# A gate matvec's weights moved from the middle of a one-core kernel to its late projection units, with a transpose step reordered

## The chip, the cores and the metric

The kernel runs on one core of a Trainium2 chip. The metric is the device time of one execution in microseconds (us), lower is better. The number compared is the median of several runs.

## What is computed

One layer (DEPTH = 1) of a hybrid block over 256 latent tokens and 256 context tokens, D_MODEL 2048. The parts that matter here:

```python
shift_l, scale_l, gate_l = adaln_modulation(c, w_mod, b_mod)      # silu(c) @ w_mod + b_mod, three 2048-wide parts
h = concat([h_ctx, h_lat])                                        # modulated RMSNorm, 512 tokens
(na_q, na_k, na_v, na_gate, pool_u, pool_gate, rw_r, rw_k, rw_v, rw_gate,
 rw_lw, rw_la, merge_logits) = split(h @ w_in)                    # three mixers and the merge gates
y_na   = neighbourhood attention (16 heads of 64)                 # keys: 256 latent + 256 context
y_pool = multi-scale pooling
y_rw   = RWKV-7 scans in both directions (16 heads of 64, 64-token chunks here)
merged = sigmoid(merge_logits) parts times (branch @ w_branch), summed over three branches
out    = x_lat + gate_l * (merged @ w_out), then a final RMSNorm
```

The "gate matvec" is the last third of the first line: silu(c) times a 2048 x 2048 slice of `w_mod`, 16 MB of weights for a single output row. It is used only at the very end, in `finish`.

## The kernel before

The first stage (to about 150 us) loads x, computes shift and scale and the first seven projection tiles. Then comes the stage of the mixers (150 to about 1390 us), in which TensorE's order of work is written out by a planner; then the branch projections (`br`, to about 1526 us) and the output projection.

In the mixers' stage the bulk of the work is projection tiles. A tile is four units; a unit is one 256 KB load `raw` (line 565), a cast to `whi` on ScalarE (568), a rest `wlo` on VectorE (569), and 12 matmuls into PSUM tile `d` (738), 256 columns wide for latent tokens or 512 for all. `raw` has 7 buffers, `whi` and `wlo` 5 each. `units()` hands out units from a list `todo`, three loads ahead of the matmuls; an entry of the list is taken when its event has been reached, and entries with no event (the 48 merge tiles, and the four tiles of the gate matvec, which stand ahead of them in the list) fill whatever time is left.

Beside the units run "streams": attention for one head pair after another (`side`), and the RWKV work per head pair p (`rwkv`): `features`, `scores`, `inverse`, `merge`, `chain`, `readout`. Each stream is a generator that yields a pair (TensorE time, time until the next step is ready); `Order.run` puts up to MOST = 2.2 us of ready steps and then at least LEAST = 0.6 us of units into the order. So the constants in the yields set how much unit work stands between two dependent steps.

`scores(p, q)` (q = 0 context, 1 latent) turns v into `pv` (230), copies it to `SV` by four ScalarE copies (235), then makes the score products `pb` and `pk` from `BK` and `EO` (248, 250), masks them on VectorE (253 to 268), and last transposes `BK` for both heads, eight transposes of head 0 into one PSUM tile `pt`, then eight of head 1 into another (276), with a ScalarE copy after each (277). All of these PSUM tiles share two buffers (tag "f"). `BK` itself is finished by `features` on VectorE (210) and ScalarE (211).

A tile of the gate matvec (`gate_tile`, 952 to 980) is 16 loads `wg` of 256 KB (957) into the `raw` buffers, [128, 512] with 2 KB rows. After each four loads follow four matmuls of 512 columns (967), one in each group of 32 columns of the array; after 16 the copy `gs` (972), the sum over the four groups `pg` (946), an add into `gb` (947) and a store to `gd` (948).

After the mixers, `bload` brings the three branches back: one buffer `bf` of 1 MB is loaded (1039), cast to `bh` on ScalarE (1042), and its rest `bl` made on VectorE (1043), three times in a row. The first matmuls of `br` need `bh0` and `bl0`, the next ones `bh1`, `bl1`, then `bh2`, `bl2`.

Of the kernel before, what the change touches and what calls it, by code (L numbers as in the profile page):

```python
# [9 lines left out]
F32 = mybir.dt.float32  # L10
# [9 lines left out]
class Rwkv:  # L20
# [90 lines left out]
    def features(s, p, q, zk, zv, T, psp, ptag, gates):  # L111


        nc, fp = s.nc, s.fp
        nm = f"{p}_{q}"
# [10 lines left out]
        k = s.mix(zk, 0, p, "k" + nm)  # L126
# [21 lines left out]
        h = 0.5 * C  # L148
# [63 lines left out]
        s.BK, s.v = BK, v  # L212
        yield 0.0, 2.6

# [6 lines left out]
    def scores(s, p, q, psp, ptag):  # L221
# [9 lines left out]
        for par in range(2):  # L231
            h = hv[1 - par]
            for d in range(2):
                o = SV[h, par, ::-1, d] if d else SV[h, par, :, d]
                nc.scalar.copy(o, pv[h])
        yield 0.6, 1.6
        v4 = lambda a: a.rearrange("p (e c) t -> p e c t", e=2)
        for g in range(1 + q):
# [25 lines left out]
            else:  # L264
                m = (s.mb, s.mk1)[g]
                for par in range(2):
                    r = hv[1 - par]
                    nc.vector.tensor_tensor(v4(EO[r, par, g]), v4(pk[r]), m[r].unsqueeze(2).to_broadcast([64, 2, 4, 64]), ALU.mult)
            yield 1.7, (2.5 if g == q else 2.2)
        s.blocks_out(p, q)  # L270

        for par in range(2):
            pt = psp.tile([128, 8, 64], F32, tag=ptag, name=f"pt{nm}_{par}")
            for c in range(8):
                src = BK[hv[par], c, par:par + 2, :].rearrange("p a t -> p (a t)")
                nc.tensor.transpose(pt[:, c], src, s.ident[hv[par], hv[par]])
            nc.scalar.copy(s.BKT[p, q][:, par], pt.rearrange("p (d c) t -> p d c t", d=2))
        yield 1.3, 0.0

# [73 lines left out]
    def chain(s, p, psp, ptag, psy, ytag, y, mark):  # L353
# [6 lines left out]
        for i in range(8):  # L360
# [16 lines left out]
            if q:  # L377
                py = psy.tile([128, 2, 64], F32, tag=ytag, name=f"py{p}_{i}")
                for d in range(2):
                    for par in range(2):  # L380
                        nc.tensor.matmul(py[hv[par], d], SV[:, par, w, d], EO[:, par, d, 4 + cs[d], :], start=(d == 0), stop=False,
                                         tile_position=(0, 64 * par), skip_group_check=True)
            yield (0.9 if q else 0.45), (0.6 if q else 1.0)
            pu = psp.tile([128, 2, 64], F32, tag=ptag, name=f"pu{p}_{i}")
# [3 lines left out]
            for par in range(2):  # L388
                (nc.scalar.copy if par else nc.vector.tensor_copy)(SV[hv[par], par, w], pu[hv[par]])
            yield 0.4, 1.3  # L390
            if i < 7:
# [139 lines left out]
def hybrid_block(ctx, tc, x, cx, w_ms, w_st, w_in, w_mg, w_br, w_out, pool_w, icnt, wa, bias, rows, params, out, dbg=None):  # L531
    nc = tc.nc
    mark = (dbg or {}).get("mark", lambda *_: None)
    P = 128
# [212 lines left out]
    with ExitStack() as mx:  # L747
# [121 lines left out]
        def attention(p):  # L869
# [10 lines left out]
            for qt in range(2):  # L880
# [35 lines left out]
                nc.vector.scalar_tensor_tensor(g[:, c], po, 0.5, g[:, c], ALU.mult, ALU.mult)  # L916
                yield 1.1, 0.3
            keep(0, p, g)
# [23 lines left out]
        def gate_out(cc, gs, gb):  # L942
            yield 0.0, 1.2
            c = slice(512 * cc, 512 * cc + 512)
            pg = psd.tile([P, 512], F32, tag="d", name=f"pg{cc}")
            nc.tensor.matmul(pg, selg, gs, start=True, stop=True)
            nc.vector.tensor_tensor(gb, pg, gb, ALU.add)
            nc.sync.dma_start(gd[:, c], gb)
            yield 1.1, 0.0

        def gate_tile(cc):

            wgs, box = {}, []

            def unit_(u):
                wg = wgs[u] = wp.tile([P, 512], F32, tag="raw", bufs=NRAW, name=f"wg{cc}_{u}")
                nc.sync.dma_start(wg, w_mg[cc, u // 2, :, u % 2])
                if u % 4 < 3:
                    return []

                def mult():
                    if not box:
                        box.append(psd.tile([P, 512], F32, tag="d", name=f"mg{cc}"))
                    a = box[0]
                    for kt in range(u - 3, u + 1):
                        g = kt % 4
                        nc.tensor.matmul(a[32 * g:32 * g + 32], cs[:, kt], wgs[kt], start=(kt < 4), stop=(kt >= 12),
                                         tile_position=(0, 32 * g))
                    if u == 15:
                        gs = wp.tile([P, 512], F32, tag="raw", bufs=NRAW, name=f"gs{cc}")  # L970
                        gb = wp.tile([P, 512], F32, tag="raw", bufs=NRAW, name=f"gb{cc}")
                        nc.scalar.copy(gs, a)
                        nc.sync.dma_start(gb, rows[0:1, 512 * cc:512 * cc + 512].to_broadcast([P, 512]))
                        O.add(gate_out(cc, gs, gb), 1)
                    return 1.4
                return [mult]
            return [lambda u=u: unit_(u) for u in range(16)]

# [4 lines left out]
        for p in range(8):  # L983
# [12 lines left out]
            if p % 2:  # L996
                for e in range(2):
                    todo.append((f"at{p}", tile_(PL_U + p - 1 + e, True, pool_u, p // 2, e)))
                for e in range(2):
                    todo.append((f"at{p}", gate_(PL_G + p - 1 + e, f"plg{p - 1 + e}", "g2p", 2)))  # L1000
            if p >= 4:
                todo.append((None, lambda cc=p - 4: gate_tile(cc)))
        for i in range(48):
            todo.append((None, tile_(MERGE + i, True, merge_out, i)))

        def units():

            ready, cur = [], []
            while True:
                while len(ready) < AHEAD:  # L1010
                    if not cur:
                        i = next((i for i, (ev, _) in enumerate(todo) if ev is None or O.has(ev)), None)
                        if i is None:
                            break
                        cur = todo.pop(i)[1]()
                    ready.append(cur.pop(0)())
                if not ready:
                    if not todo:
                        return
                    yield None  # L1020
                    continue
                for m in ready.pop(0):
                    yield m()
# [161 lines left out]
```

## Time and profile before

| | us |
|---|---|
| median of 3 runs (lowest to highest) | 1617.97 (1617.08 to 1625.06) |
| profiled execution, its own time | 1624.09 |
| its span, first to last instruction | 1622.2 |
| TensorE (PE) busy | 1544.7 |
| VectorE (DVE) busy | 1140.2 |
| ScalarE (ACT) busy | 813.6 |
| granted TensorE clock, mean | 0.990 |

PE is TensorE's matmuls, PEld its weight loads, SP the engine that issues the DMAs. A profile row gives the start or the busy time first, then the engine, the line of the kernel, the operation and its tiles. A busy PE need not be at its peak: ends of matmuls are modelled, and a group of matmuls in which one waits for a load still counts as busy in part. A wait is put down to the event that came last.

### The profile page before, as it was taken

What the parts mean: (1) busy time and instruction counts of PE and PEld (TensorE: products, weight loads), DVE (VectorE), ACT (ScalarE), POOL (GpSimd) and SP (SyncE); (2) the same over time, 40 slices, a digit from 0 to 9 for tenths busy, and PEclk for the clock granted to TensorE, in tenths of its full rate; (3) what the DMA queues carried; (4) which work ended last, traced back from release to release, by engine and by line L of the source; (5) the groups of instructions that cost most, each with busy time, mean ns of one, the idle gap of its engine ahead of it and who ended that gap; (6) DMA issues with size and microseconds to landing.
All of it is one profiled execution on the core that took longest, in us unless ns stands there. A gap on an engine that the chain in (4) does not pass through costs nothing.

```text
span 1622.2 us, 36488 instructions
## 1 busy us (share of the span) xinstructions
PE 1544.7 (95%) x13848; PEld 1314.9 (81%) x13848; DVE 1140.2 (70%) x2585; ACT 813.6 (50%) x1604; POOL 248.5 (15%) x441
## 2 busy tenths in 40 slices
PE   6999989899999998998999999999899999999998
PEld 4667747388887887877888897787799999999987
DVE  4334875588688788778768878968886554677774
ACT  5224732455364466446446546536644554444553
POOL 2222200140031023023014214003312100000000
PEclk9999999999999999999999999999999999999999
DMA  9997376754433433442442452342366486677892
GB/s 380 331 337 237 111 224 201 231 166 156 144 99 104 146 111 107 134 125 73 137 125 85 153 173 86 105 147 83 106 184 191 163 259 231 221 231 233 271 310 74
DMA packets 201617, 283.26 MB, mean 175 GB/s; under 512 B 67809, under 2 KB 97633, under 8 KB 196833
## 3 DMA queue, kind: packets, MB, share of 16 engines
q1 hardware_dynamic: 201440, 280.93, 53.7%
q8 instruction: 109, 1.79, 0.4%
q14 instruction: 68, 0.55, 0.1%
HBM read 262.24 MB, written 18.35 MB: 173 GB/s over the span
## 4 chain that ended last, share of the span: by engine, by line
PE 78%; DVE 8%; DMA 5%; ACT 4%; issue 3%; SPq 1%; POOL 0%; ACTq 0%; DVEq 0%
PE d L738 43%; PE br L574 3%; PE br L575 3%; PE br L576 3%; PE acc L662 2%; PE psm L614 2%; PE o L574 2%; PE o L575 2%; PE o L576 2%; DMA wg<-in_w_mg 2%; PE acc L665 2%; PE acc L668 2%; DVE wlo L569 2%; DMA bf<-bs 1%; PE pu L387 1%
## 5 line engine op out<-in xcount | busy, mean ns | idle before, releaser
L738 PE MATMUL d<-hh,whi 128*128 128x256 f32 (+1 forms) x1952 | 573.7, 318 | 2.4 <-ACT whi L568 2.2
L568 ACT CAST whi<-raw 128x512 fp32r<-128x512 f32 x584 | 358.5, 620 | 421.8 <-PE d L738 287.5
L738 PE MATMUL d<-hl,whi 128*128 128x256 f32 (+1 forms) x1952 | 553.1, 307 | 0.0
L569 DVE TENSOR_TENSOR wlo<-raw,whi 128x512 fp32r<-128x512 f32 x584 | 404.0, 700 | 175.2 <-ACT whi L568 125.9
L738 PEld LDWEIGHTS d<-hh,whi 128*128 128x128 f32 x1952 | 369.8, 189 | 35.6 <-issue 5.6
L738 PEld LDWEIGHTS d<-hl,whi 128*128 128x128 f32 x1952 | 370.5, 190 | 17.6 <-issue 0.2
L738 PE MATMUL d<-hh,wlo 128*128 128x256 f32 (+1 forms) x1952 | 365.5, 308 | 2.9 <-DVE wlo L569 2.8
L738 PEld LDWEIGHTS d<-hh,wlo 128*128 128x128 f32 x1952 | 287.1, 190 | 22.3 <-DVE wlo L569 3.9
L369 POOL TENSOR_SCALAR sg<-SV,G 64x64 f32<-64x64 f32 x192 | 107.3, 564 | 275.2 <-DVE SV L404 139.5
L574 PE MATMUL br<-bh,whi 128*128 128x256 f32 x384 | 107.9, 281 | 0.0
L575 PE MATMUL br<-bl,whi 128*128 128x256 f32 x384 | 107.9, 281 | 0.0
L576 PE MATMUL br<-bh,wlo 128*128 128x256 f32 x384 | 107.9, 281 | 0.0
L308 DVE TENSOR_TENSOR iM<-iA,iT 128x126 f32<-128x126 f32 (+22 forms) x248 | 65.2, 263 | 12.1 <-DMA iA<-dA 5.6
L576 PEld LDWEIGHTS br<-bh,wlo 128*128 128x128 f32 x384 | 72.4, 188 | 0.0
L574 PEld LDWEIGHTS br<-bh,whi 128*128 128x128 f32 x384 | 72.4, 188 | 0.0
L575 PEld LDWEIGHTS br<-bl,whi 128*128 128x128 f32 x384 | 72.4, 188 | 0.0
L310 DVE TENSOR_TENSOR iT<-iT,iM 128x126 f32<-128x126 f32 (+22 forms) x248 | 64.2, 259 | 6.4
L675 ACT ACTIVATE hh<-xT,md 128x256 fp32r<-128x256 f32 x32 | 17.5, 594 | 88.9 <-DVE md L634 88.9
L1113 DVE TENSOR_TENSOR hl<-rawo,hh 128x512 fp32r<-128x512 f32 x64 | 42.6, 689 | 21.8 <-ACT hh L1112 21.5
L1112 ACT CAST hh<-rawo 128x512 fp32r<-128x512 f32 x64 | 39.3, 621 | 33.2 <-DMA rawo<-in_w_out 15.9
L575 PE MATMUL o<-hl,mh 128*128 128x512 f32 (+1 forms) x144 | 52.6, 366 | 0.0
L574 PE MATMUL o<-hh,mh 128*128 128x512 f32 (+1 forms) x144 | 52.6, 365 | 0.0
(283 smaller groups left out, 2286.6 us busy)
## 6 DMA issues: line engine op xcount, KB each, us to landing
raw<-in_w_in SPq DMA_DIRECT2D x488, 256.0 KB, 3.3
wm<-in_w_ms SPq DMA_DIRECT2D x32, 1024.0 KB, 6.8
raw<-in_w_br SPq DMA_DIRECT2D x96, 256.0 KB, 3.2
wg<-in_w_mg SPq DMA_DIRECT2D x64, 256.0 KB, 4.6
rawo<-in_w_out SPq DMA_DIRECT2D x64, 256.0 KB, 4.3
wst<-in_w_st SPq DMA_DIRECT2D x16, 448.0 KB, 7.5
md__79<-mth SPq DMA_DIRECT2D x48, 128.0 KB, 2.7
mth<-md__79 SPq DMA_DIRECT2D x48, 128.0 KB, 3.1
```

Source lines behind the costliest of these rows:

```text
L308: nc.vector.tensor_tensor(m, A[:, st:st + 1, st + 1:32].to_broadcast([128, ni, nt]), T[:, 0:ni, st:st + 1].to_broadcast([128, ni, nt]), AL ...
L310: nc.vector.tensor_tensor(T[:, 0:ni, st + 1:32], T[:, 0:ni, st + 1:32], m, ALU.add)
L369: nc.gpsimd.tensor_scalar(sg[hv[par], d], SV[hv[par], par, w, d], G[hv[par], gs[d][0], d:d + 1], None, ALU.mult)
L568: nc.scalar.copy(h, raw)
L569: nc.vector.tensor_tensor(l, raw, h.bitcast(F32), ALU.subtract)
L574: nc.tensor.matmul(acc, a[0], b[0], start=start, stop=False)
L575: nc.tensor.matmul(acc, a[0], b[1], start=False, stop=False)
L576: nc.tensor.matmul(acc, a[1], b[0], start=False, stop=stop)
L614: mm = nc.tensor.matmul(psm[j][32 * g:32 * g + 32, 0:256], cs[:, kt], wm[:, k], start=(kt < 4), stop=(kt >= 12), tile_position=(0, 32 * g))
L738: nc.tensor.matmul(box[0], w[m >= 8][:, 128 * i:128 * i + 128], x, start=(u == 0 and m == 0), stop=(u == 3 and m == 11))
L1112: nc.scalar.copy(hh[kt], raw)
L1113: nc.vector.tensor_tensor(hl[kt], raw, hh[kt].bitcast(F32), ALU.subtract)
```

## The change

Three things. (1) The gate matvec no longer has tiles of its own in `todo`. Its weights come in 64 pieces [128, 2, 256] of 256 KB (rows of 1 KB), into four buffers that attention used (`kt`, `PT`), one piece with each projection unit that is handed out after attention and pooling of the last pair are over (event `side7`). After each second piece follow four matmuls of 256 columns. `gs` and `gb` move into attention's `sl` buffers, and the PSUM tiles into attention's. (2) In `scores` the transposes stand ahead of the score products, and the two heads alternate. (3) Constants in yields are changed.

```diff
 features:
-        yield 0.0, 2.6
+        yield 0.0, (3.6 if q == 0 else 4.8)
 scores:
                 nc.scalar.copy(o, pv[h])
-        yield 0.6, 1.6
+        yield 0.6, 1.2
+
+        pt = [psp.tile([128, 8, 64], F32, tag=ptag, name=f"pt{nm}_{par}") for par in range(2)]
+        for c in range(8):
+            for par in range(2):
+                src = BK[hv[par], c, par:par + 2, :].rearrange("p a t -> p (a t)")
+                nc.tensor.transpose(pt[par][:, c], src, s.ident[hv[par], hv[par]])
+        for par in range(2):
+            nc.scalar.copy(s.BKT[p, q][:, par], pt[par].rearrange("p (d c) t -> p d c t", d=2))
+        yield 0.9, 1.6
...
-            yield 1.7, (2.5 if g == q else 2.2)
+            yield 1.3, 2.6
         s.blocks_out(p, q)
-
-        for par in range(2):
-            pt = psp.tile([128, 8, 64], F32, tag=ptag, name=f"pt{nm}_{par}")
-            for c in range(8):
-                src = BK[hv[par], c, par:par + 2, :].rearrange("p a t -> p (a t)")
-                nc.tensor.transpose(pt[:, c], src, s.ident[hv[par], hv[par]])
-            nc.scalar.copy(s.BKT[p, q][:, par], pt.rearrange("p (d c) t -> p d c t", d=2))
-        yield 1.3, 0.0
 chain:
-            yield (0.9 if q else 0.45), (0.6 if q else 1.0)
+            yield (0.9 if q else 0.45), (0.7 if q else 1.2)
...
-            yield 0.4, 1.3
+            yield 0.4, 1.6
 attention:
-                yield 1.1, 0.3
+                yield 1.1, 1.0
 gate_out:
-            pg = psd.tile([P, 512], F32, tag="d", name=f"pg{cc}")
+            pg = psn.tile([P, 512], F32, tag="o", name=f"pg{cc}")
-        def gate_tile(cc):
...
-                wg = wgs[u] = wp.tile([P, 512], F32, tag="raw", bufs=NRAW, name=f"wg{cc}_{u}")
-                nc.sync.dma_start(wg, w_mg[cc, u // 2, :, u % 2])
-                if u % 4 < 3:
+        def gate_units():
...
+            def load(cc, h, k):
+                wg = np_.tile([P, 2, 256], F32, tag=("kt", "PT")[k // 2 % 2], bufs=2, name=f"wg{cc}_{h}_{k}")
+                nc.sync.dma_start(wg, w_mg[cc, k, :, :, 256 * h:256 * h + 256])
+                held.append(wg)
+                if k % 2 == 0:
                     return []
...
+                    for i in range(4):
+                        kt = 2 * k - 2 + i
                         g = kt % 4
-                        nc.tensor.matmul(a[32 * g:32 * g + 32], cs[:, kt], wgs[kt], start=(kt < 4), stop=(kt >= 12),
-                                         tile_position=(0, 32 * g))
+                        nc.tensor.matmul(a[32 * g:32 * g + 32], cs[:, kt], held[i // 2][:, i % 2], start=(kt < 4), stop=(kt >= 12),
+                                         tile_position=(0, 32 * g), skip_group_check=True)
...
-                    return 1.4
+                    return 0.75
 todo:
-            if p >= 4:
-                todo.append((None, lambda cc=p - 4: gate_tile(cc)))
 units:
                         cur = todo.pop(i)[1]()
+                        if O.has("side7") and gates:
+                            cur = [lambda u=u, g=gates.pop(0): u() + g() for u in cur]
```

How the order of instructions moves, at three places.

TensorE, gate matvec. Before, the matmuls `mg` of a gate tile stand among the attention and RWKV steps of pairs 0 and 1 (`po`, `pg`, `S`), with no unit between (here the last gate tile):

```order
L946 MATMUL pg2_3150<-gs2_3136,selg_128 128x512
L967 MATMUL mg3_3162<-wg3_0_3128,cs_74 32x512
L967 MATMUL mg3_3162<-wg3_1_3130,cs_74 32x512
L967 MATMUL mg3_3162<-wg3_2_3154,cs_74 32x512
L967 MATMUL mg3_3162<-wg3_3_3156,cs_74 32x512
L887 MATMUL S1_0_1_3169<-kh1_2707,qh1_2602 128x512
```

Now they stand between the units of the last 20 projection tiles, a pair of pieces after every second unit (`d109` is a merge tile, `whi410` belongs to unit 410 of 488):

```order
L739 MATMUL d109_15987<-hh6_87,wlo410_15954 128x256
L739 MATMUL d109_15987<-hh7_88,wlo410_15954 128x256
L970 MATMUL mg0_16024<-wg0_0_0_15933,cs_74 32x256 x2
L970 MATMUL mg0_16024<-wg0_0_1_15957,cs_74 32x256 x2
L739 MATMUL d109_15987<-hh8_89,whi411_15981 128x256
L739 MATMUL d109_15987<-hl8_105,whi411_15981 128x256
```

The first pair follows unit 410, the last one unit 472; 16 units are left after it, and then `br` begins.

TensorE, the transposes of `scores` for pair 7, q = 1. Before, they come after `pb` and `pk`, head after head:

```order
L738 MATMUL d39_15061<-hh2_83,whi353_14973 128x256
L738 MATMUL d39_15061<-hl2_99,whi353_14973 128x256
L276 MATMUL pt7_1_0_15072<-ident_63,BK7_1_14610 128x64 x8
L276 MATMUL pt7_1_1_15082<-ident_63,BK7_1_14610 128x64 x8
L738 MATMUL d39_15061<-hh3_84,whi353_14973 128x256
```

Now they come between `pv` and `pb`, one of head 0 and one of head 1 in turn, sixteen rows of which these are the first:

```order
L739 MATMUL d39_15533<-hh2_83,wlo393_15427 128x256
L739 MATMUL d39_15533<-hh3_84,wlo393_15427 128x256
L242 MATMUL pt7_1_0_15556<-ident_63,BK7_1_15208 128x64
L242 MATMUL pt7_1_1_15557<-ident_63,BK7_1_15208 128x64
L242 MATMUL pt7_1_0_15556<-ident_63,BK7_1_15208 128x64
L242 MATMUL pt7_1_1_15557<-ident_63,BK7_1_15208 128x64
```

Between `pv` and the first transpose of head 1 stand 12 to 20 unit matmuls in most of the 16 cases, and between the last transpose and `pb` about as many.

SP, the first load of `bload`. Before, `bf0` is issued soon after the last RWKV result `grwg7` is stored, with 52 units still to load:

```order
L764 DMA bs_80<-grwg7_15261 128x256 [waits DMAHW1_49,DVE_49]
L565 DMA raw433_17030<-in_w_in 128x512 [waits DMAHW2_49,DVE_49]
L565 DMA raw434_17048<-in_w_in 128x512 [waits DMAHW3_49,DVE_49]
L565 DMA raw435_17069<-in_w_in 128x512 [waits DMAHW4_49,DVE_49]
L829 DMA md__79<-mth31_16914 128x256 [waits DMAHW5_49,Activation_49]
L565 DMA raw436_17088<-in_w_in 128x512 [waits DMAHW6_49,DVE_49]
L1039 DMA bf0_18137<-bs_80 128x8x256 [waits DMAHW7_49,PE_49,Pool_49]
```

Now it stands behind the store of the last gate part (`gd` from `gb3`) and waits for that queue slot (DMAHW3), with one unit left to load:

```order
L977 DMA gb3_17886<-in_rows 128x512 [waits DMAHW0_49]
L566 DMA raw484_18064<-in_w_in 128x512 [waits DMAHW1_49,DVE_49]
L566 DMA raw485_18082<-in_w_in 128x512 [waits DMAHW2_49,DVE_49]
L949 DMA gd_78<-gb3_17886 128x512 [waits DMAHW3_49,DVE_49]
L566 DMA raw486_18100<-in_w_in 128x512 [waits DMAHW4_49,DVE_49]
L566 DMA raw487_18121<-in_w_in 128x512 [waits DMAHW5_49,DVE_49]
L1044 DMA bf0_18201<-bs_80 128x8x256 [waits DMAHW6_49,DMAHW3_49,PE_49]
```

## Rows read from the trace of the kernel before

**Rows 1.** The page: busy time, share of the span and instructions of each engine; then the chain of work that ended last, shares of the span by engine.
```profile
PE 1544.7 (95%) x13848; PEld 1314.9 (81%) x13848; DVE 1140.2 (70%) x2585; ACT 813.6 (50%) x1604; POOL 248.5 (15%) x441
...
PE 78%; DVE 8%; DMA 5%; ACT 4%; issue 3%; SPq 1%; POOL 0%; ACTq 0%; DVEq 0%
```

**Rows 2.** Busy time by stretch: from:to, its length, then busy us (instructions) of each engine, granted clock in the stretch, mean busy share of the 16 DMA engines, GB/s.
```profile
200.00:325.00 125.00, 110.90 (x832) 67.68 (x831) 76.10 (x189) 46.00 (x97) 5.38 (x18) 0.97 0.69 215
...
900.00:1050.00 150.00, 147.20 (x1408) 123.38 (x1407) 123.20 (x302) 84.88 (x172) 33.06 (x53) 1.00 0.42 127
...
1296.00:1332.00 36.00, 33.91 (x278) 32.92 (x277) 18.45 (x23) 19.39 (x31) 0.00 (x0) 1.00 0.83 271
```

**Rows 3.** Waits of TensorE's matmuls from 150 to 1390 us: who waited for whom, us in total, times, longest.
```profile
PE pb L250 <- DVE BK L210: 8.9, 5, 2.4
PE mg L967 <- DMA wg<-in_w_mg: 6.7, 8, 1.4
PE S L887 <- DVE gnag L916: 4.6, 4, 1.8
PE pS L397 <- ACT SV L389: 4.4, 7, 1.6
PE pu L387 <- DVE xs L376: 4.1, 7, 1.2
PE pg L946 <- ACT gs L972: 3.6, 3, 1.5
...
PE pb L250 <- ACT BK L211: 3.2, 5, 0.8
...
PE pk L248 <- ACT SV L235: 0.8, 1, 0.8
...
PE pk L250 <- ACT SV L235: 0.3, 1, 0.3
```

**Rows 4.** The gate matvec's matmuls (line 967) alone: the last line of the busy time by stretch from 200 to 325 us (sum over the stretches); then, from the view of tile `wg`, the time from issue to landing of its loads.
```profile
sum 125.00, PE 37.41 PEld 6.13; mean PE 6.23 PEld 1.02
...
DMA to landing us min/median/max: 2.5/4.6/6.6
```

**Rows 5.** Timeline of TensorE at the gate matvec: start, length, instruction, count, and the idle time ahead of it with its releaser.
```profile
207.75 1.06 PE L967 MATMUL mg<-wg,cs 128*32 128x512 f32 x8
208.74 0.66 PE L905 MATMUL pt<-ident,sl 128*128 128x128 f32 x4
...
305.34 1.05 PE L967 MATMUL mg<-wg,cs 128*32 128x512 f32 x4
307.71 1.72 PE L967 MATMUL mg<-wg,cs 128*32 128x512 f32 x4 [1.32 <-DMA wg<-in_w_mg]
309.36 0.50 PE L887 MATMUL S<-kh,qh 64*128 64x512 f32 x2
```

**Rows 6.** Timeline of TensorE in the first stage, where the shift and scale matvec (`psm`) has the shape that the gate matvec will have.
```profile
23.31 1.93 PE L614 MATMUL psm<-wm,cs 128*32 128x256 f32 x32
...
30.75 0.40 PE L662 MATMUL acc<-hh,shi 128*128 128x512 f32 x1
30.99 0.40 PE L665 MATMUL acc<-hh,slo 128*128 128x512 f32 x1
31.22 0.63 PE L668 MATMUL acc<-hl,shi 128*128 128x512 f32 x2
31.78 1.07 PE L614 MATMUL psm<-wm,cs 128*32 128x256 f32 x16
32.78 0.50 PE L662 MATMUL acc<-hh,shi 128*128 128x512 f32 x1
33.12 0.40 PE L665 MATMUL acc<-hh,slo 128*128 128x512 f32 x1
```

**Rows 7.** Timeline of TensorE: attention scores, whose two heads alternate, and behind them one set of 16 transposes of line 276.
```profile
218.04 0.39 PE L887 MATMUL S<-kl,qh 64*128 64x512 f32 x2
218.27 0.40 PE L887 MATMUL S<-kh,ql 64*128 64x512 f32 x2
218.51 0.95 PE L276 MATMUL pt<-ident,BK 64*128 64x64 f32 x16
219.40 1.93 PE L967 MATMUL mg<-wg,cs 128*32 128x512 f32 x8
```

**Rows 8.** The view of line 235 (copies of `pv` to `SV`): duration in ns, min/median/max.
```profile
L235 ACT COPY SV<-pv x64: 348/367/370, 178.4 to 1156.4; 64x256 f32<-64x256 f32 x64
```

**Rows 9.** Timelines: the end of the last gate tile (ScalarE, TensorE, VectorE, SP); then `bload` from the issue of `bf0` to the last `bl`. Last, the DMA view's line of the stores to `gd`: count, KB each, median us to landing.
```profile
321.71 0.58 ACT L972 COPY gs<-mg 128x512 f32<-128x512 f32 x1
...
325.41 0.33 SPq L948 DMA_DIRECT2D gd<-gb  x1
...
1296.72 0.38 SPq L1039 DMA_DIRECT2D bf<-bs  x1
...
1329.64 2.29 DVE L1043 TENSOR_TENSOR bl<-bf,bh 128x2048 fp32r<-128x2048 f32 x1 [5.57 <-ACT bh L1042]
...
gd<-gb SPq DMA_DIRECT2D x4, 256.0 KB, 3.0
```

**Rows 10.** Busy time by stretch, columns as in rows 2: merge units alone; `bload` beside units (two stretches); the gate matvec's loads; the stores of the inverse and the loads of its result; then, from the DMA view, the line of the x loads (count, KB each, median us to landing).
```profile
1340.00:1385.00 45.00, 45.00 (x383) 45.00 (x382) 21.78 (x33) 22.39 (x41) 0.00 (x0) 1.00 0.67 221
...
1296.70:1305.50 8.80, 8.80 (x76) 8.80 (x76) 3.46 (x5) 2.94 (x7) 0.00 (x0) 1.00 0.96 311
...
1321.00:1327.00 6.00, 6.00 (x53) 6.00 (x52) 3.07 (x6) 1.08 (x2) 0.00 (x0) 1.00 0.96 276
...
290.00:300.00 10.00, 7.42 (x45) 2.47 (x41) 2.44 (x8) 1.46 (x3) 1.74 (x4) 1.00 0.84 237
...
1209.60:1212.40 2.80, 2.80 (x26) 2.80 (x25) 2.67 (x5) 1.48 (x3) 0.00 (x0) 1.00 0.94 213
1212.50:1216.40 3.90, 3.90 (x36) 3.90 (x35) 0.23 (x1) 1.57 (x4) 0.00 (x0) 1.00 0.70 170
...
xt<-in_x SPq DMA_DIRECT2D x2, 1024.0 KB, 10.1
```

More of the change, by code (lines that the diff above doesn't have):

```diff
@@ L949, in gate_out @@
             yield 1.1, 0.0
-        def gate_tile(cc):
-            wgs, box = {}, []
-            def unit_(u):
-                wg = wgs[u] = wp.tile([P, 512], F32, tag="raw", bufs=NRAW, name=f"wg{cc}_{u}")
-                nc.sync.dma_start(wg, w_mg[cc, u // 2, :, u % 2])
-                if u % 4 < 3:
+        def gate_units():
+            held = []
+            def load(cc, h, k):
[3 more added lines that the diff above has]
+                if k % 2 == 0:
@@ L959, in unit_ @@
                     return []
                 def mult():
[L962 to L965, printed above, removed]
-                        g = kt % 4
-                        nc.tensor.matmul(a[32 * g:32 * g + 32], cs[:, kt], wgs[kt], start=(kt < 4), stop=(kt >= 12),
-                                         tile_position=(0, 32 * g))
[L969 to L972, printed above, removed]
+                    if h == 0 and k == 1:
+                        T["mg"] = psn.tile([P, 512], F32, tag="s", name=f"mg{cc}")
@@ new lines, in mult @@
+                    a = T["mg"][:, 256 * h:256 * h + 256]
+                    for i in range(4):
+                        kt = 2 * k - 2 + i
+                        g = kt % 4
+                        nc.tensor.matmul(a[32 * g:32 * g + 32], cs[:, kt], held[i // 2][:, i % 2], start=(kt < 4), stop=(kt >= 12),
+                                         tile_position=(0, 32 * g), skip_group_check=True)
+                    del held[0:2]
+                    if h == 1 and k == 7:
+                        gs = np_.tile([P, 512], F32, tag="sl", bufs=2, name=f"gs{cc}")
+                        gb = np_.tile([P, 512], F32, tag="sl", bufs=2, name=f"gb{cc}")
+                        nc.scalar.copy(gs, T["mg"])
@@ L973, in mult @@
                         nc.sync.dma_start(gb, rows[0:1, 512 * cc:512 * cc + 512].to_broadcast([P, 512]))
                         O.add(gate_out(cc, gs, gb), 1)
-                    return 1.4
+                    return 0.75
                 return [mult]
-            return [lambda u=u: unit_(u) for u in range(16)]
+            return [lambda cc=cc, h=h, k=k: load(cc, h, k) for cc in range(4) for h in range(2) for k in range(8)]
         todo = []
@@ L1006, in units @@
         def units():
-            ready, cur = [], []
+            ready, cur, gates = [], [], gate_units()
             while True:
@@ L1018, in units @@
                     if not todo:
+                        assert not gates
                         return
```

## The prediction

> **What bounds the kernel now.** I read the page first, then the busy time by stretch, the waits of TensorE, and the timelines at the places that the change touches. TensorE is busy for 1544.7 of 1622.2 us and makes 78% of the chain that ended last [rows 1]. So a change gains what it takes from TensorE's own time or from the holes in it. Unit work without an event is always at hand to fill holes, but only where the written order puts it. The stretch from 200 to 325 us is the weakest of the mixers' stage: 110.90 busy of 125, against 147.20 of 150 from 900 to 1050 [rows 2]. In it lies the whole gate matvec.
>
> The sum is made against the profiled execution, 1624.09 us. The median of the runs shown is 6.1 us (0.4%) lower, and I carry the difference over. A measurement of this kernel can tell about 0.5% (8 us) from no change.
>
> **Gate matvec, taken out of 200 to 325 us.** Its matmuls fill 37.4 us [rows 4]; TensorE is idle for 6.7 us more until a `wg` load lands and 3.6 us until `gs` is copied [rows 3]. Together 47.7 us. Much of the 37.4 is waiting too: with its data there a group of four matmuls takes 1.0 us (207.75 to 208.74), while another takes 4.0 (305.34 to 309.36) [rows 5], so 16 groups need only some 16 us. Removed: 47.7.
>
> **Gate matvec, put back between late units.** 32 pairs of pieces, each four matmuls of 256 columns. The trace before has this shape only in `psm`. There eight matmuls (16 records) start 0.09 us late (31.78, where 31.22 + 0.24 + 0.23 was due), take 1.00 us, and the next interval is 0.34 instead of 0.23: 1.20 us per visit. Another group with 32 records takes 1.93 instead of 1.07, so eight records fewer save 0.43 [rows 6]. A pair then costs 0.77 us and 32 of them 24.5. The ends: 0.43 without any cost at the edges (14 us) and 1.0, the group of 512 columns (32 us). I take the `psm` row, which is the same shape. The Trainium skill (TensorEngine Tiling (Array Packing), Key Properties) says that changing the tiling mode drains TensorE, which speaks against cutting the matvec into twice as many visits; the late start and the long interval in `psm` agree with it. Without that rule, by the body of the group alone, the sum would gain about 6 us more. To the 24.5 I add 2 us for the four `pg`, each of which waits about half a us for its `gs` (0.58 us [rows 9]) half a unit behind the last pair. Net of the two parts: 47.7 - 24.5 - 2 = **21.2 saved**.
>
> **Transposes.** A set of 16 takes 0.89 us (218.51 to 219.40), one after another. Attention's scores have the same split of the rows into two halves and alternate heads: there a pair of 512-column matmuls takes 0.23 us (218.04 to 218.27) [rows 7], as much as a single one of that width in rows 6 (30.75 to 30.99). If the two halves overlap as they do there, each of the 16 sets loses half: 16 x 0.445 = **7.1 saved**. The ends are 0 and 7.1; I take the upper one because the row is the same tile shape.
>
> **More units ahead of the waits.** Behind `BK` the first step that needs it stood 2.6 + 0.6 + 1.6 = 4.8 us later by the planner's count; for q = 1 it is now 4.8 + 0.6 + 1.2 = 6.6. The waits on `BK` are 8.9 and 3.2 us, five each, longest 2.4 [rows 3]; 1.8 us more ahead of them removes about **9** (0 to 12). The waits for `gnag`, `SV` and `xs` are 4.6, 4.4 and 4.1 us [rows 3]; their yields grow by 0.7, 0.3 and 0.1 to 0.2 us, and I count **4** (0 to 13).
>
> **A new wait.** The second PSUM buffer for the transposes is that of `pv`, and comes free after four copies of 0.37 us, 1.5 us in all [rows 8], plus whatever ScalarE has ahead of them (a cast of 0.62). Before, `pk` met the same wait, for only 0.8 and 0.3 us [rows 3], with more units ahead. Now 12 unit matmuls of 0.1175 us (45 us / 383 [rows 10]), 1.4 us, often stand there. Behind the waiting transpose stands all of TensorE. 16 times 0.4 is **6 lost** (0 to 13).
>
> **The late units and their loads.** From unit 409 to 472 TensorE has 64 units of 12 x 0.1175 = 1.41 us (90 us), the 24.5, and some 19 us of `pg`, the last pair's chain, merge and readout (an estimate of mine, by their groups' counts): 134 us, or 4.2 per pair of units. The DMAs have 128 loads of 256 KB, 16 stores of 128 KB and six transfers for `gb` and `gd`: 37.2 MB, and the inverse of pair 7, whose last two steps fill all engines for 2.6 and 2.7 us (0.94 x 2.8, 0.70 x 3.9 [rows 10]); with its first steps about 8, an estimate. The pieces have rows of 1 KB, as `bf` has. Beside `bf` the DMAs moved 311 GB/s at a share of 0.96 and 276 at 0.96, beside units alone 221 at 0.67 [rows 10], that is 324, 288 and 330 at full share. So the loads need 115 to 129 us plus 8, 123 to 137, against TensorE's 134. They are about level, so the loads no longer hide in all stretches: **6 lost** (0 to 31, the upper end in a rival below). The Trainium skill (DMA: Bandwidth & Descriptors, Specifications) puts the smallest transfer for line rate at 512 B, so by it 1 KB rows cost nothing, and at 330 GB/s this term would be 0; the row with 276 GB/s at 0.96 says otherwise, and I go by the rows.
>
> **What is late next: `bload`.** Before, `bf0` was issued at 1296.72 with over 50 units left, and the last `bl` was done 35.2 us later (1329.64 + 2.29) [rows 9] with only 2.1 us of idle TensorE (36 - 33.91 [rows 2]). Now `bf0` waits for the store of the last gate part. That store was issued at 325.41, 3.7 us after `gs` began at 321.71, and takes 3.0 to land [rows 9]: with the drain before `gs`, `bf0` starts 7.1 us after the last pair, and `bl2` is done at 7.1 + 35.2 = 42.3. TensorE has left 16 units (22.6), `pg` (0.6), and the first two branches' 48 matmuls (5.7), 28.9 us. It misses 13.4; less the 2.1 lost before: **11.2 lost** (5 to 17). Nothing can fill this, since all units are used up.
>
> **Sum.** Saved 21.2 + 7.1 + 9 + 4 = 41.3, lost 6 + 6 + 11.2 = 23.2: 18.1 us. 1624.09 becomes 1606.0, and on the runs' level 1617.97 - 18.1 = **1600 us**.
>
> **Rivals.**
> - *The tail costs nothing.* Loads stay ahead and units still cover `bload`. For: TensorE and DMAs are level in the middle estimate, and raw loads run some ten units ahead. Against: `bf0` really stands behind `gd` in SP's order. Then 17.2 us more are saved: 1583.
> - *The loads set the pace of the tail.* The old gate loads, issued in a row, moved only 237 GB/s from 290 to 300 us [rows 10]. At that rate 37.2 MB take 157 us, with the inverse 165, 31 more than TensorE's 134 in place of 6: the sum becomes +6.9, or 1625, no change that can be told. The moved weights would give back what the middle gained.
> - *Slower: the loop of four buffers.* A pair of pieces can be loaded only when the pair before the last has been multiplied, so two pairs pass per landing plus 0.77. At the landing times of before (median 4.6, longest 6.6 [rows 4]) that is under 4.2 us per pair and costs nothing. Two loads of raw and two of `wg` now share the queue, though, and 1 MB x loads in the busy first stage took 10.1 us to land [rows 10]. At 10.1 a pair takes 5.44, 1.25 more than 4.19: 40 us instead of 6, so the sum is 15.8 slower, 1634. It decides from a landing of 9.1 us on, where the other terms' 24.1 us are used up (24.1 / 32 = 0.75 per pair). Against it: the DMAs catch up while TensorE waits.
> - *The change doesn't do what it says* in one part: the two halves' transposes don't overlap. Then 7 less, 1607; this stays inside the forecast's own range.
>
> **How the numbers follow.** The forecast with its bounds (1588 to 1611): 0.47, nearly all of it faster by over 0.5% (below 1609.9). The free tail: 0.17, faster. The loads' pace: 0.20, within 0.5%. The slower loop: 0.13, and 0.03 for something else on that side, half of it within. So faster 0.63, same 0.23, slower 0.14. The range runs from 1581, just below the free tail, to 1625, the loads' pace; beyond it lie the slower loop and a few hundredths of a better outcome.
>
> **What would show it.** Right: from 200 to 325 us TensorE is over 97% busy and no row of `wg` is left there; pairs of `mg` take about 0.8 us; sets of transposes take 0.45; waits on `BK` fall below 4 us; the idle time ahead of `br` lies with `bf`, `bh` or `bl` and is 9 to 15 us; `wg` lands in 4 to 7 us. Wrong: over 20 us of TensorE's idle time put down to `wg`, a landing over 9 us, or a transposes' wait of more than 0.8 us each on `SV`. If `br` begins without a wait, the term for `bload` was wrong.

## The result and the profile after

The changed kernel takes 1595.37 us (median of 4 runs, 1594.43 to 1598.03) beside 1618.68 for the kernel before (4 runs): a ratio of 0.9851, 95% interval 0.9822 to 0.9881. That is 23.3 us faster by the medians. The profiled execution of it takes 1594.74 us, that of before 1624.09, so the two traces differ by 29.4 us; 5.4 of these are the profiled execution of before being above its median.

The page of the changed kernel, busy time and then the chain that ended last:

```profile
PE 1520.5 (95%) x13976; PEld 1309.4 (82%) x13976; DVE 1132.3 (71%) x2585; ACT 815.9 (51%) x1606; POOL 242.3 (15%) x441
...
PE 78%; DVE 9%; DMA 5%; ACT 4%; issue 2%; POOL 1%; SPq 1%; ACTq 0%; DVEq 0%; POOLq 0%
```

Beside [rows 1] the bound is the same: TensorE is busy for 24.2 us less in a span 29.2 us shorter. Busy time by stretch, columns as in [rows 2]:

```profile
200.00:325.00 125.00, 122.15 (x1282) 109.96 (x1281) 104.95 (x253) 70.18 (x149) 16.34 (x36) 1.00 0.49 149
...
1332.00:1480.00 148.00, 139.19 (x1152) 138.26 (x1152) 102.60 (x180) 70.28 (x116) 0.00 (x0) 0.98 0.75 236
```

The weak stretch has become full (110.90 before), with 450 more instructions of TensorE in the same 125 us. A new hole of 8.8 us has opened behind 1332. Waits of TensorE's matmuls from 150 to 1400 us, columns as in [rows 3]:

```profile
PE br L575 <- ACT bh L1047: 5.6, 1, 5.6
PE mg L970 <- DMA wg<-in_w_mg: 5.2, 5, 2.1
PE pt L242 <- DVE BK L210: 4.8, 2, 3.5
PE pk L259 <- DVE EO L277: 3.6, 4, 1.4
PE pS L398 <- ACT SV L390: 3.5, 3, 1.5
PE pu L388 <- DVE xs L377: 3.1, 6, 0.7
...
PE pt L242 <- ACT SV L235: 2.8, 4, 1.4
...
PE pt L242 <- ACT BK L211: 1.7, 3, 0.7
PE br L576 <- DVE bl L1048: 1.5, 1, 1.5
...
PE S L888 <- DVE gnag L917: 0.3, 1, 0.3
```

The waits on `BK` stand with the transposes now and fell from 12.1 to 6.5; `gnag` fell from 4.6 to 0.3. The two at `br` (7.1) are new; with 1.7 us just ahead of it (`whi` and `wlo` late at 1344 and 1346 us) they are the 8.8. All waits from 150 to 1400 us sum to 53.4 us before and 48.0 after. So most of the difference between the traces is TensorE's own time: its busy time on the gate's products fell from 37.4 to 25.5 us and on the transposes from 18.8 to 14.4, and the clock, below, cost 6.6 us less.

One visit to a pair of gate pieces in TensorE's timeline:

```profile
1320.61 0.39 PE L739 MATMUL d<-hh,wlo 128*128 128x256 f32 x2
1320.93 0.64 PE L970 MATMUL mg<-wg,cs 128*32 128x256 f32 x8
1321.50 0.39 PE L739 MATMUL d<-hh,whi 128*128 128x256 f32 x1
1321.72 0.28 PE L739 MATMUL d<-hl,whi 128*128 128x256 f32 x1
```

Two unit matmuls from 1320.61 would have let the pair start at about 1320.84; it starts 0.09 late, takes 0.57, and the next interval is 0.22 instead of 0.12. That makes 0.76 us, as `psm` in [rows 6] let expect (0.77). The Trainium skill (TensorEngine Tiling (Array Packing), Key Properties) has TensorE drain at a change of the tiling mode; the two longer intervals agree with it.

The end of the gate matvec, SP's timeline of the changed kernel, and then VectorE's one row there that waits:

```profile
1325.48 1.00 SPq L977 DMA_DIRECT2D gb<-in_rows  x1
1326.58 2.40 SPq L566 DMA_DIRECT2D raw<-in_w_in  x2
1330.76 0.33 SPq L949 DMA_DIRECT2D gd<-gb  x1
1331.36 0.93 SPq L566 DMA_DIRECT2D raw<-in_w_in  x2
1333.44 0.38 SPq L1044 DMA_DIRECT2D bf<-bs  x1
```

```profile
1330.04 0.69 DVE L948 TENSOR_TENSOR gb<-pg,gb 128x512 f32<-128x512 f32 x1 [1.42 <-DMA gb<-in_rows]
```

The last pair begins at 1324.54, and `bf0` is issued 8.9 us behind that. Some of it is `gb` itself: its load is issued only behind the last pair and lands 4.6 us later.

What the prediction has no term for is TensorE's clock. Busy time of TensorE by stretch (then granted clock, DMA share, GB/s), first in the kernel before, then in the changed one:

```profile
230.00:232.00 2.00, 1.20 (x8) 0.92 0.95 342
232.00:234.00 2.00, 1.49 (x7) 0.50 0.93 329
234.00:236.00 2.00, 2.00 (x11) 0.50 0.35 122
236.00:238.00 2.00, 2.00 (x10) 0.50 0.21 68
```

```profile
1360.00:1362.00 2.00, 0.00 (x0) 0.92 1.08 370
1362.00:1364.00 2.00, 0.00 (x0) 0.50 1.04 377
1364.00:1366.00 2.00, 1.72 (x8) 0.50 0.84 310
1366.00:1368.00 2.00, 2.00 (x11) 0.50 0.06 23
1368.00:1370.00 2.00, 2.00 (x17) 0.87 0.19 67
```

Both fall to the lower level (0.50, which is 1.2 of 2.4 GHz) behind a wait: at 230 TensorE had stood for 1.82 us, at 1362 it stands in the 5.6 us for `bh`. Work goes on at half speed for some us after the wait has ended. I took such stretches one us at a time from 150 to 1500 us and summed busy time times (1 - granted clock): 12.8 us in the kernel before, 6.2 in the changed one. The Trainium skill (TensorE: Matmul & The Clock Gate, Part 1) lets half or all of the clock through by how busy the array has lately been; these rows agree.

The 6.6 us between them are a matter of these two executions, though, and not of the two kernels. Every execution's mean granted clock is on record: 0.991 to 0.993 in the four of the changed kernel, and a median of 0.992 (0.985 to 0.995) in the 43 of the kernel before that the runs below were timed against. The profiled one of before has 0.990.

### The profile page after: what moved, and what is told of

Same layout as the page of the kernel before. It is cut to its first block, busy times and chain, and to the rows that moved or that the text cites. A ratio compares the mean times of both kernels' runs of the same rounds, so it can differ in the third digit from the quotient of the medians.

```text
span 1593.0 us, 36719 instructions
## 1 busy us (share of the span) xinstructions
PE 1520.5 (95%) x13976; PEld 1309.4 (82%) x13976; DVE 1132.3 (71%) x2585; ACT 815.9 (51%) x1606; POOL 242.3 (15%) x441
## 4 chain that ended last, share of the span: by engine, by line
PE 78%; DVE 9%; DMA 5%; ACT 4%; issue 2%; POOL 1%; SPq 1%; ACTq 0%; DVEq 0%; POOLq 0%
PE d L739 43%; PE br L575 3%; PE br L577 3%; PE br L576 3%; PE acc L663 2%; PE psm L615 2%; PE o L577 2%; PE o L575 2%; PE o L576 2%; DMA wg<-in_w_mg 2%; PE acc L669 2%; PE acc L666 2%; DVE wlo L570 1%; PE pu L388 1%; DMA bf<-bs 1%
## 5 line engine op out<-in xcount | busy, mean ns | idle before, releaser
L1117 ACT CAST hh<-rawo 128x512 fp32r<-128x512 f32 x64 | 39.5, 621 | 33.0 <-PE o L577 23.3
L624 DVE COPY ms<-psm 128x256 f32<-128x256 f32 x16 | 6.8, 425 | 65.1 <-PE psm L615 65.1
```

Source lines behind the costliest of these rows:

```text
L1117: nc.scalar.copy(hh[kt], raw)
```

## Experiments

Each was timed beside the kernel before on its chip (1620.1 to 1621.7 us there); ratios are to it.

**The parts, one at a time.** Four runs: the gate's edits alone, the rest of the change alone, the new order of the scores alone, the other pauses alone. Their edits, hunks of the change on top of the kernel before (`e2` on the change, with the gate's undone):

```
e1 (the reverse of this, on the change, is e2)
-            if p >= 4:
-                todo.append((None, lambda cc=p - 4: gate_tile(cc)))
+            ready, cur, gates = [], [], gate_units()
...
+                        if O.has("side7") and gates:
+                            cur = [lambda u=u, g=gates.pop(0): u() + g() for u in cur]
e3
-        yield 0.6, 1.6
+        yield 0.6, 1.2
+        pt = [psp.tile([128, 8, 64], F32, tag=ptag, name=f"pt{nm}_{par}") for par in range(2)]
...
-            yield 1.7, (2.5 if g == q else 2.2)
+            yield 1.3, 2.6
e4
-        yield 0.0, 2.6
+        yield 0.0, (3.6 if q == 0 else 4.8)
-            yield (0.9 if q else 0.45), (0.6 if q else 1.0)
+            yield (0.9 if q else 0.45), (0.7 if q else 1.2)
-            yield 0.4, 1.3
+            yield 0.4, 1.6
-                yield 1.1, 0.3
+                yield 1.1, 1.0
```

> The kernel before with the gate matvec's weights moved to the late units and nothing else (scores and yields as before). My theory, with the terms as the changed kernel's profile shows them: 47.7 us of gate work and waits leave the middle, 24.5 + 2 come back late, about 5 us of waits on wg and 7 us of bload are lost, so 9 to 13 us faster than before. Rival A (the late loads eat the whole gain, and the gain of the change comes from the reordered scores and the yields): within 4 us of before. Rival B (the gate move is the whole gain): 20 to 25 us faster.

> The changed kernel with the gate matvec back in the middle as four tiles of its own; transposes of scores and all yields stay changed. My theory: 10 to 15 us faster than before (fewer waits on BK, gnag, SV, xs). Rival A: 20 to 25 us faster, all of the gain. Rival B: within 4 us of before.

> The kernel before with scores as in the change (transposes of both heads in turn, ahead of the score products, with the yields inside scores), all other yields and the gate as before. If alternating heads overlapped, 16 sets would lose half of 0.89 us and it would be 5 to 7 us faster. The changed kernel's profile shows a set at 0.94 us still, so my theory now is no gain from the overlap, and waits on BK that move from pb to pt: within 3 us of before.

> The kernel before with only the yields of features, chain and attention changed; scores and gate as before. My theory: the waits on BK (12 us), gnag, SV and xs (13 us) shrink, 8 to 14 us faster. Rival: these waits are replaced by others of the same length, within 3 us of before.

Gate alone: 0.9916 (0.9888 to 0.9944), 13.6 us faster. The rest: 0.9908 (0.9891 to 0.9924), 14.9. Order: 0.9952 (0.9936 to 0.9969), 7.8; this I had expected to be nothing, from a set of 0.94 us that in fact holds a wait for `SV` behind its first transpose (at 1148.7 us in the changed kernel; most sets without a wait take 0.59 to 0.73). Pauses: 1.0001 (0.9987 to 1.0015), nothing, where I had expected 8 to 14. So gate and rest both count, and add up within the noise (28.5 beside 24.2 for the change by its ratio).

Why the pauses alone take nothing off can be read from the waits of `e4`:

```profile
PE mg L967 <- DMA wg<-in_w_mg: 9.9, 10, 2.0
...
PE pb L250 <- ACT BK L211: 2.5, 5, 0.7
...
PE pb L250 <- DVE BK L210: 2.2, 2, 1.5
```

The waits that the pauses were meant for did fall: on `BK` from 12.1 to 4.7 us, on `gnag`, `SV` and `xs` together from 13.1 to 5.3. But others grew, on `wg` from 6.7 to 9.9, and all of them from 150 to 1400 us sum to 53.2 beside 53.4. The rival held. And the granted clock is lower, 0.987 to 0.990 (median 0.989) in all 11 executions of `e4`; the trace has 16.2 us lost to it, 12.8 before. With the order, the pauses came out 7 ahead of the order alone (`e2` beside `e3`); the runs below return to that.

**The gate's price in both kernels.** The matvec left out of the changed kernel (`e6`) and of the kernel before (`e7`); the gate row then holds its bias alone.

```
-            ready, cur, gates = [], [], gate_units()
+            ready, cur, gates = [], [], []
...
+            nc.sync.dma_start(gb, rows[0:1, 512 * cc:512 * cc + 512].to_broadcast([P, 512]))
+            nc.sync.dma_start(gd[:, 512 * cc:512 * cc + 512], gb)
```

> The changed kernel without the gate matvec: the gate row holds its bias alone and is written at the start, so 256 products, their 64 loads and the row's sums are left out. My theory (the gate costs its own 32 pair visits of 0.76 us, 24.3 us, five waits of 5.2 us on pieces and about 6 us of the wait for the bias row at the end): 33 to 38 us faster than the changed kernel, 1557 to 1562 us beside 1595. Rival (the gate's products stand in gaps that TensorE would spend waiting for other engines): under 25 us. Other rival (its 16.8 MB also delay the projection's loads): over 42 us.

> The kernel before without the gate matvec, left out in the same way. My theory (there the gate costs its four groups at 11.9 us each, 47.7 us, and 2.1 us at the end): 46 to 51 us faster than the kernel before, about 1570 us. Then the gate's price has fallen by 13 us from the kernel before to the changed one, as the gate alone moved did in its own run. Rival (the groups partly fill waits of attention): under 38 us, and then the gain of moving the gate comes from elsewhere.

`e7`: 0.9714 (0.9690 to 0.9737), so the gate costs 46.4 us in the kernel before (47.2 by the medians, 1574.49 beside 1621.73). `e6`: 0.9612 (0.9593 to 0.9630), 1558.94; against the change's 0.9851 that is 38.8 us, some 6 either way by the intervals, a little over the 33 to 38 expected and far from the 25 of the first rival.

The parts can be found in the traces. The 32 visits make 24.3 and the sums over bands 4.4 busy. Late pieces cost about twice the 5.2 us that the matmuls' waits show, since the modelled ends of the matmuls cover the rest: the weight loads ahead of them (PEld) waited for 10.1 us (the changed kernel's view of tile `wg`), and the visits that met a late piece were longer by about that much.

```profile
  PEld mg L970: 10.1, 12
```

Of the 8.8 us at the end 4.9 go, since without a gate TensorE still waits at `br` for 3.9. But `e6` has 4.8 us in two casts where the mixers' stage begins, behind its early loads of the gate's rows (last row; the change has none there). `e7` has such a wait too.

```profile
PE br L575 <- ACT bh L1052: 2.5, 1, 2.5
...
PE br L576 <- DVE bl L1053: 1.4, 1, 1.4
...
PE d L739 <- ACT whi L569: 4.8, 2, 3.7
```

Together 24.3 + 4.4 + 10.1 + 4.9 - 4.8 = 38.9. The price fell by 7.6 us, beside 9 from `e2` to the change: the visits save some 23 us, and the late pieces and the end take most of that back. The gate alone gained more (13.6); with the old pauses, 480 unit matmuls stand behind the last pair, and `br` begins without a wait for `bh` or `bl`.

**The pauses.** The changed kernel with the old pause behind the features (`e13`), and with all four pauses of the list of `e4` at their old values (`e14`).

```
e13
-        yield 0.0, (3.6 if q == 0 else 4.8)
+        yield 0.0, 2.6
e14, the same line and the other three pairs of e4 reversed
-            yield 0.4, 1.6
+            yield 0.4, 1.3
...
```

> The changed kernel with the pause behind the features at its old 2.6 instead of 3.6 and 4.8; all other edits stay. The pauses alone moved nothing on the kernel before, but with the new order of the scores they came out 7 us ahead of the new order alone. My theory (the new order puts the transposes, which read BK, where BK is not yet written, and this longer pause is what covers that): 4 to 7 us slower, with waits of the transposes on BK of 11 us as in the run of the scores' order alone, beside 6.5 in the changed kernel. Rival (the gain comes from the pauses of the chain and of attention): within 2 us.

> The changed kernel with all of its lengthened pauses at their old values: behind the features, in the chain and in attention. What is left of the change is the gate's move and the new order of the scores. Alone these two gained 13.6 and 7.8 us. The old pause behind the features alone came out at 1592.0 us, no slower than the change. My theory (the pauses of the chain and of attention carry the 7 us by which order and pauses together were ahead of the order alone): 3 to 7 us slower than the changed kernel's 1595.4 us, 1598 to 1602. Rival (the pauses move waits from one place to another and carry nothing that lasts): 1591 to 1596 us.

`e13`: 1591.97 us, 0.9822 (0.9799 to 0.9846). `e14`: 1595.83 us, 0.9844 (0.9820 to 0.9868), the change's own time. My theory fell in both: in the changed kernel the pauses carry nothing. The waits of `e14` from 150 to 1400 us show why:

```profile
PE pu L388 <- DVE xs L377: 5.9, 7, 2.0
PE pt L242 <- DVE BK L210: 5.3, 4, 2.0
PE pt L242 <- ACT BK L211: 4.9, 5, 1.5
PE pt L242 <- ACT SV L235: 4.5, 3, 1.8
...
PE mg L970 <- DMA wg<-in_w_mg: 1.4, 1, 1.4
```

and the first row of `br` in it, from the view of that tile (ns min/median/max, first and last start):

```profile
L575 PE MATMUL br<-bh,whi x384: 277/281/358, 1359.5 to 1495.6; 128*128 128x256 f32 x192
```

The mixers wait more (all waits from 150 to 1170 us sum to 36.8, 32.2 with the change's pauses) and the clock loses 10.0 us instead of 6.2: 8.4 us for the pauses in these two traces. (The clock's part is not seen in all executions, with medians of 0.992 and 0.9915.) But no wait at `br` is left: from 1340 to 1500 us all waits come to 0.2, beside 8.8. The written order says where these 8.6 went. Between the last gate product and the first of `br` stand 384 unit matmuls with the old pauses, 192 with the new (240 in `e13`, 480 with the gate alone). A longer pause puts more units ahead of the mixers' steps; units spent there are missing as cover for the branches that `bload` brings back. The two cancel in the traces; the times say that less than some 6 us is left, by the intervals. `e2` beside `e3` fits this: with the gate in the middle `bf0` is issued as late as in the change (1333.46 us), but 274 unit matmuls still follow before `br`, and 2.2 us of waits are all that stands there. So the pauses could keep their 7 us.

**Alternating or not.** The changed kernel with its transposes ahead of the scores, head after head.

```
-        for c in range(8):
-            for par in range(2):
+        for par in range(2):
+            for c in range(8):
```

> The changed kernel with its transposes of BK still ahead of the score products, but eight of one head and then eight of the other, as the kernel before had them. In the traces a set of sixteen without a wait inside took 0.95 us before and 0.64 us in the changed kernel. My theory (the two row halves partly overlap when they alternate, 0.3 us a set on 16 sets): 4 to 6 us slower than the changed kernel. Rival (the sets stand beside waits that end no sooner, so that their length matters little): within 2 us.

1599.57 us (1597.41 to 1602.35), 0.9872 (0.9848 to 0.9895): 4.2 us above the change by the medians, at the lower end of my 4 to 6; the intervals of the two ratios overlap. The trace is plainer. TensorE's groups (busy us, mean ns | idle before) of `e12`, then the same row of the changed kernel:

```profile
L242 PE MATMUL pt<-ident,BK 64*128 64x64 f32 x256 | 19.2, 232 | 6.2 <-DVE BK L210 4.7 <-ACT SV L235 1.0 <-ACT BK L211 0.4
```

```profile
L242 PE MATMUL pt<-ident,BK 64*128 64x64 f32 x256 | 14.4, 236 | 9.4 <-DVE BK L210 4.8 <-ACT SV L235 2.8 <-ACT BK L211 1.7
```

4.8 us of TensorE's own time, 0.30 a set. One set of the changed kernel in the timeline takes 0.64 us where [rows 7] had 0.89:

```profile
974.10 0.71 PE L242 MATMUL pt<-ident,BK 64*128 64x64 f32 x16
974.74 0.33 PE L388 MATMUL pu<-xs,AT 64*64 64x64 f32 x4
```

**The tail.** Three runs on the changed kernel: pieces in rows of 2 KB (`e5`), the branches' first load `bf0` early (`e10`), the bias row early (`e11`).

```
e5
-                nc.sync.dma_start(wg, w_mg[cc, k, :, :, 256 * h:256 * h + 256])
+                nc.sync.dma_start(wg, w_mg[cc, h, k])
e10
-                        gs = np_.tile([P, 512], F32, tag="sl", bufs=2, name=f"gs{cc}")
+                        gs = wp.tile([P, 512], F32, tag="raw", bufs=NRAW, name=f"gs{cc}")
...
+        with tc.high_priority(offset=(300 if br == 0 else 0)):
e11
+                if h == 1 and k == 1:
+                    T["gb"] = np_.tile([P, 512], F32, tag="sl", bufs=2, name=f"gb{cc}")
+                    nc.sync.dma_start(T["gb"], rows[0:1, 512 * cc:512 * cc + 512].to_broadcast([P, 512]))
```

> The changed kernel with the gate's weights laid out so that a half's piece is read in rows of 2 KB where the change reads rows of 1 KB; the order of work and the bytes are the same. My theory (the tail's loads stand late because the changed pieces move slower: 2.9 us median and 7.2 us longest from issue to landing in the changed kernel's trace): the waits of the gate's products on their pieces (5.2 us in five waits) fall under 2.5 us and the time falls by 2 to 4 us. Rival (the late pieces are late because their buffers come free late and because the whole queue is full, not because of the row): waits and time stay within 1.5 us.

> The changed kernel with the first load of the gated bias issued right behind the last piece of the gate's weights, ahead of the last projection loads, and with the row's sum and bias in the projection's load buffers instead of the slices'. My theory (TensorE stands idle 8.0 us at the end of the projection since the first bias load is issued 8.3 us after the last pair of the gate, behind loads that wait for buffers): the idle time there falls to 2 to 4 us and the time by 4 to 6 us. Rival (the early load and its split on ScalarE stand in front of projection loads and splits, which then come late): the wait moves to the last projection units, within 2 us either way.

> The changed kernel with the load of a column group's bias row issued with the second half's second piece instead of behind the group's last product. In the changed kernel's trace the last group's sum over bands is done at about 1326.5 us, but the addition of the bias waits for its row, which was issued at 1325.48 and landed at 1330.04; the gate row's write, and the first load of the gated bias that waits for it, follow. My theory (this load holds up the chain behind the last pair by about 3.5 us): the wait of the bias products on bh (5.6 us) falls to 2 to 3 us and the time by 2 to 4 us. Rival (the gated bias's load then waits for projection loads ahead of it on the queue instead): within 1.5 us.

What the last two expectations call the gated bias are the branches, `bf` and `bh`; the bias row is `gb`. In the first of the three, 2.9 us is the shortest time to landing and not the median, which is 4.1.

`e5`: 1593.71 us, 0.9825 (0.9807 to 0.9843), not to be told from the change. The rival held: TensorE's wait on pieces stayed (first row, from its waits), and the time from issue to landing (second row, from the view of tile `wg`) changed little from the 2.9/4.1/7.2 of the change. The weight loads waited for 8.9 us, beside 10.1. What did change is the time that SP takes to issue one piece: a median of 0.38 us, beside 0.56.

```profile
PE mg L970 <- DMA wg<-in_w_mg: 5.8, 5, 2.8
```

```profile
DMA to landing us min/median/max: 2.6/3.9/6.1
```

`e10`: 1605.60 us, 0.9899 (0.9876 to 0.9922), 8 (by the ratios) to 10 us (by the medians) slower than the change. The wait at `bh` went, as the theory had it, but the rival took more: the load and its split now stand in front of projection loads and their casts. Of TensorE's waits there:

```profile
PE d L739 <- ACT whi L569: 11.5, 8, 4.5
```

Eight waits for casts, up to 4.5 us at once, stand where the change has one of 0.7.

`e11`: 1587.77 us (1585.16 to 1593.35), 0.9804 (0.9775 to 0.9832), the fastest that still makes the gate, and 7.6 us below the change by the medians; the intervals of the two ratios just overlap. Its waits of TensorE:

```profile
PE br L575 <- ACT bh L1048: 4.3, 1, 4.3
...
PE mg L973 <- DMA wg<-in_w_mg: 0.3, 1, 0.3
```

and SP's timeline behind its last pair, whose last product begins at 1320.5:

```profile
1323.51 0.33 SPq L949 DMA_DIRECT2D gd<-gb  x1
1324.39 1.75 SPq L566 DMA_DIRECT2D raw<-in_w_in  x2
1326.53 0.38 SPq L1045 DMA_DIRECT2D bf<-bs  x1
```

`bf0` is issued 6.0 us behind that product, 8.6 in the change (1324.8 to 1333.44). At `br` this took 2.4 us off (7.1 to 4.7, with 0.4 at `bl` and `wlo`). More came from the waits on pieces, which I had not expected to move: 5.2 to 0.3, and 10.1 to 2.5 for the weight loads. Some 2 us of other waits came back in the mixers. The early `gb` shifted what stands on SP's queue around the first pieces; which transfer had held them, I did not separate.

## Why the prediction held, point by point

The direction and the time held (1600 forecast, 1595.4 measured); 18.1 us were forecast and 23.3 came. By the traces the saved terms come to 23.3 + 4.8 + 5.6 + 6.2 = 39.9 us (41.3 forecast) and the lost ones to 1.7 + 10.1 + 6.7 = 18.5 (23.2), each worked out below. Single terms were off by up to 4.5 us either way, so that the sum came this close is in part luck.

- **The gate taken out**, 47.7: `e7` measured 46.4. **Put back**, 24.5: 32 visits of 0.76 are 24.3. The 2 us for `pg` were too much; its waits sum to 0.1.
- **Transposes**, 7.1: 4.8 by `e12`. The rival without overlap falls, but a set takes 0.64, not 0.45. The step that took attention's 512-column scores for the measure was too hopeful.
- **Waits on `BK`**, 9: 12.1 to 6.5 is 5.6. **Other yields**, 4: `gnag`, `SV` and `xs` lost 6.2 together. But for `gnag` the reason was wrong: with the old pauses (`e14`) its wait is gone too, and only the rest comes back. And `e4` shows that less waiting at these places need not be less waiting in all.
- **The new wait on `SV`**, 6: 2.8, of which 1.1 stood before `pk` already: 1.7 more.
- **Late loads**, 6: 5.2 by the matmuls' waits, but 10.1 by those of the weight loads. From the first pair to the last (1178.7 to 1324.5) went 146 us, where the prediction has 134 and these 6. So the term was too small, and its reason did not hold: I let 1 KB rows slow the loads down, and `e5` shows no effect of them. The Trainium skill (DMA: Bandwidth & Descriptors, Specifications) asks for 512 B at least; here the page was right and I had overruled it with one row. With the same rows the weight loads wait 2.5 us in `e11` and 2.0 in `e14`; what holds them in the change is not shown.
- **`bload`**, 11.2: TensorE stood 7.1 at `br` and 1.7 for a cast and a rest ahead of it, 6.7 more than before, and some 2.1 us went to the lower clock behind it. The step counted 16 units left, which the written order confirms. It charged them to the gate's move, though: by `e14` and `e1` it is the longer pauses that leave so few, and `e6`, which has no gate, still waits 3.9 there.
- **Left out**: the clock. 6.6 us less are lost to it in the trace of the change (12.8 to 6.2). But the traces differ by 6 us more than the medians do, and over all executions the mean granted clock is the same (0.9915 and 0.992), so it does not explain why more was gained than forecast. With 39.9 - 18.5 = 21.4 the terms above come near the 23.3 without it.

Of the signs named beforehand, the full stretch (97.7% busy), the visits (0.76) and the landings (median 4.1) came; the sets (0.64), the waits on `BK` (6.5, not under 4) and the idle time ahead of `br` (8.8, not 9 to 15) did not.

Of the rivals, the free tail fell (waits of 5.2 and 8.8 stand there), the loads did not set the pace (10.1 us of waits where that rival had 31), and the loop of four buffers needed landings of 9.1 us, where 7.2 was the longest.

What stays open: what held the first pieces before `e11`, and why other waits grow and the clock falls where a pause takes some waits away (`e4`). The waits are read from one execution of each kernel.

## What to carry to other kernels

Filler is a stock: before lengthening a pause that a filler covers, count what that filler was to cover later; here the mixers' waits fell by 5 us and 9 us of waits came back at the end. When a step moves to the end, follow its result through to whoever reads it, and look for loads on that way that nothing forces to be late: the bias row, issued earlier, took 2.4 us off the wait at `br`, and more off waits that I had not thought of. Read a wait of TensorE from its weight loads too: the matmuls' rows showed half of what late pieces cost. A loop that revisits a narrow tile shape pays its edges at every visit, so price them from a row of the same shape.

## What the runs showed of the hardware

- A wait of TensorE can cost more than its length: granted clock fell to 0.50 behind waits of 1.8 and 5.6 us, and matmuls of 256 columns then started 0.21 us apart (1365.30, 1365.51 in the changed kernel) in place of 0.12. Not every such wait does it: behind two of 2.1 us (to 1188.1 and 1212.3 in the changed kernel) the granted clock stayed at 1.00.
- Transposes of 64 rows that alternate between the two halves of the rows took 0.64 us for 16, against 0.89 [rows 7] to 0.95 (382.44 to 383.39 in the kernel before) head after head: some 30% less, not half.
- Loads of 256 KB in rows of 1 KB and of 2 KB landed alike (median 4.1 and 3.9 us) at a busy share of about 0.8 (0.82 and 0.84), but SP took 0.56 and 0.38 us to issue one.
